# Three element-wise products of an RWKV-7 half on Pool, its bonus weight on ScalarE

## The chip, the cores and the metric

One core of a Trainium2 chip runs the whole program. The metric is the device time in microseconds; the median of several runs of one kernel is compared with that of the other. An engine is named by its usual name or by the profile's: TensorE (PE, with PEld for its weight loads), VectorE (DVE), ScalarE (ACT), Pool (POOL), SyncE (SP).

## What is computed

A two-layer encoder over 256 frames of width 2048: layer 0 mixes tokens with RWKV-7 and Mamba-2 heads side by side, layer 1 with chunked attention, and each ends with a SwiGLU feed-forward. The change touches the RWKV part alone, of which this is the reference, cut:

```python
kk = heads(k * k_k)
kk = kk * lax.rsqrt(jnp.maximum(jnp.sum(kk * kk, axis=-1, keepdims=True), 1e-24))
k = k * (1.0 + (a - 1.0) * k_a)
a_vec = -kk
b_vec = kk * heads(a)
def step(S, inp):
    r_t, w_t, k_t, v_t, a_t, b_t = inp
    sa = jnp.einsum('bhvk,bhk->bhv', S, a_t)
    S = S * w_t[:, :, None, :] + sa[..., None] * b_t[:, :, None, :] + v_t[..., None] * k_t[:, :, None, :]
    return S, jnp.einsum('bhvk,bhk->bhv', S, r_t)
...
bonus = jnp.sum(heads(r) * heads(k) * r_k, axis=-1, keepdims=True) * heads(v)
return (y + bonus.reshape(Bsz, T, RWKV_WIDTH)) * g
```

Here `a` is the in-context rate, `k` the key, `r` the receptance, `r_k` the bonus weight, one number per channel.

## The kernel before

The kernel keeps activations on the chip and streams all weights from HBM in units of 256 x 512 numbers. `stream` (L225 to L243) loads a unit, and for each half of it ScalarE casts a high part `hi` (L240) and VectorE subtracts it to get the low part `lo` (L241). `mm_chunk` (L245) multiplies: for each weight tile and each of two token tiles three matmuls, `hi` by `sh` (L260), `lo` by `sh` (L261), `hi` by `sl` (L262). They are called the streamed matmuls below; `hi_w_in_3_1` is the second half of unit 3 of a chunk. The tiles `hi` and `lo` come from a ring of five, so a cast waits until TensorE has used the tile five places earlier.

The input projection `w_in` has twelve chunks of 512 columns. The RWKV heads are worked in two halves (`rwkv_half`, hf 0 and 1), each with a chunk for key, receptance and value (`which` 0, 1, 2). The chunk's result is evacuated to `tm` by ScalarE, transposed by TensorE to channels by time (`tr`, L424), and mixed with the frame before: ScalarE scales (L429), VectorE adds the shifted part (L430). After the key, ScalarE and VectorE build the rate `a` (128 x 1024), the cumulated decay `c` (its inverse exponential in the end) and the normed key `kk`; L553 to L561 fill the operands `ar` and `bkv`. `bkv` holds per channel and chunk of 64 frames three blocks: the rate-weighted key (L556), the key by rate and decay (L560, L561), the value (L504 to L509). After the receptance, L564 multiplies it into `ar`, L567 forms the bonus product in `r`, and the `aa` matmuls (L576) make the 64 x 64 interactions of four chunks from `bkv` and `ar`; VectorE masks them into `AA` (L580). There are two PSUM banks for `aa`, and each chunk takes both. The triangular inverse follows: VectorE transposes `AA` to `NB` (L591), runs 30 dependent pairs of small instructions (L595, L597), and transposes again to `Sf` and `TG` (L623, L626); then TensorE's `ga` (L634), `gb`, and the recurrence over the chunks (`cx`, `cu`, `ch`, `cy`). The bonus is summed over a head by `bo` (L605). The second half's inverse runs beside the first chunks of the Mamba part (`tr_cv`, L769 convolution steps on VectorE, `xt`, L827 on Pool, `sg`, `yd`).

Each engine runs its instructions in the order in which the framework's scheduler has put them, by priorities (`high_priority`, the stream above the mixer) and its own estimate of durations. An instruction that waits holds all behind it on its engine. Tiles of 128 x 1024 (`r4`) are reused from a pool of nine.

Of the kernel before, what the change touches and what calls it, by code (L numbers as in the profile page):

```python
# [12 lines left out]
AF = mybir.ActivationFunctionType  # L13
ALU = mybir.AluOpType
# [128 lines left out]
def encoder_body(ctx: ExitStack, tc: tile.TileContext, A):  # L143
    nc = tc.nc
    act, dve, pool, pe = nc.scalar, nc.vector, nc.gpsimd, nc.tensor
# [58 lines left out]
    def col(name, i=0, rows=P):  # L204
        return pf[:rows, _PF[name] + i:_PF[name] + i + 1]
# [187 lines left out]
    def mixer0(xt):  # L393
# [5 lines left out]
        with ExitStack() as mx:  # L399
# [76 lines left out]
            def c64(ap):  # L476
                return ap.rearrange("p q (c t) -> p (q c) t", t=64)
# [3 lines left out]
            def rwkv_half(hf):  # L481
                f0 = 4 * hf
# [4 lines left out]
                k = r4(f"k{hf}")  # L487
                r = r4(f"r{hf}")
                bkv = R1.tile([P, 16, 192], F32, tag="bkv", name=f"bkv{hf}")
                for which in range(3):  # L490
                    tm = proj(1 + 3 * hf + which)
                    for q2 in range(2):
                        ps = tr2(tm, [256 * q2, 256 * q2 + 128], P, f"{which}{hf}{q2}")
                        for i in range(2):
                            q = 2 * q2 + i
# [4 lines left out]
                            else:  # L500
# [4 lines left out]
                                               scale=om[:, mi:mi + 1])  # L505
# [4 lines left out]
                                                         op0=ALU.mult, op1=ALU.add)  # L510
                    if which == 0:

                        lw = r4(f"lw{hf}")
                        a = r4(f"a{hf}")
                        for wi, dst in ((0, lw), (1, a)):
                            for q2 in range(2):
                                ps = pra.tile([P, 2, T], F32, tag="ra", name=f"lo{hf}{wi}{q2}")
                                for i in range(2):
                                    q = 2 * q2 + i
                                    pe.matmul(ps[:, i, :], lhsT=w2[:, wi, q * P:(q + 1) * P], rhs=wa[:, wi, :],  # L520
                                              start=True, stop=True)
                                for i in range(2):
                                    q = 2 * q2 + i
                                    b0 = 8 * wi + f0 + q
                                    act.activation(dst[:, q, :], ps[:, i, :], AF.Tanh, scale=0.5,
                                                   bias=hw0[:, b0:b0 + 1])
                        act.activation(lw, lw, AF.Identity, scale=-0.5 * CW, bias=ncw)
                        c = r4(f"c{hf}")
                        for q in range(4):
                            dve.tensor_tensor_scan(c[:, q, :], scan_m, lw[:, q, :], 0.0, op0=ALU.mult, op1=ALU.add)  # L530
                        dve.tensor_tensor(lw, c, lw, op=ALU.subtract)
                        kk = r4(f"kk{hf}")
                        for q in range(4):
                            act.activation(kk[:, q, :], k[:, q, :], AF.Square, scale=col("k_k", f0 + q))
                        for q2 in range(2):
                            ps = pra.tile([P, 2, T], F32, tag="ra", name=f"ss{hf}{q2}")
                            pe.matmul(ps, lhsT=blk, rhs=kk[:, 2 * q2:2 * q2 + 2, :], start=True, stop=True)
                            dve.tensor_scalar(kk[:, 2 * q2:2 * q2 + 2, :], ps, 1e-24, None, op0=ALU.max)
                        act.activation(kk, kk, AF.Ln)
                        act.activation(kk, kk, AF.Exp, scale=-0.5)  # L540
                        for q in range(4):
                            dve.scalar_tensor_tensor(kk[:, q, :], k[:, q, :], col("k_k", f0 + q), kk[:, q, :],
                                                     op0=ALU.mult, op1=ALU.mult)

                        ar = [r4(f"ar{hf}{i}", shape=(P, 8, 128)) for i in range(2)]
                        wt = R2.tile([P, 16], F32, tag="wt", name=f"wt{hf}")
                        act.activation(wt, c64(c)[:, :, 63], AF.Exp)
                        act.activation(lw, lw, AF.Exp)
                        for i in range(2):
                            act.activation(ar[i][:, :, 64:128], c64(c[:, 2 * i:2 * i + 2, :]), AF.Exp)  # L550
                        act.activation(c, c, AF.Exp, scale=-1.0)
                        for i in range(2):
                            dve.scalar_tensor_tensor(ar[i][:, :, 0:64], c64(kk[:, 2 * i:2 * i + 2, :]), -1.0,  # L553
                                                     c64(lw[:, 2 * i:2 * i + 2, :]), op0=ALU.mult, op1=ALU.mult)
                        dve.scalar_tensor_tensor(kk, a, 1.0, kk, op0=ALU.add, op1=ALU.mult)
                        dve.scalar_tensor_tensor(bkv[:, :, 0:64], c64(kk), 0.5, c64(c), op0=ALU.mult, op1=ALU.mult)  # L556
                        for q in range(4):
                            act.activation(a[:, q, :], a[:, q, :], AF.Identity, scale=hka[:, f0 + q:f0 + q + 1],
                                           bias=oka[:, f0 + q:f0 + q + 1])
                        dve.tensor_tensor(a, a, k, op=ALU.mult)  # L560
                        dve.tensor_tensor(bkv[:, :, 64:128], c64(a), c64(c), op=ALU.mult)  # L561
                    elif which == 1:
                        for i in range(2):
                            dve.tensor_tensor(ar[i][:, :, 64:128], c64(r[:, 2 * i:2 * i + 2, :]),  # L564
                                              ar[i][:, :, 64:128], op=ALU.mult)
                        for q in range(4):
                            dve.scalar_tensor_tensor(r[:, q, :], r[:, q, :], col("r_k", f0 + q), a[:, q, :],  # L567
                                                     op0=ALU.mult, op1=ALU.mult)

                        AA = R1.tile([P, 32, 128], F32, tag="AA", name=f"AA{hf}")  # L570
                        for ch in range(4):
                            pss = [pra.tile([P, 4, 128], F32, tag="ra", name=f"aa{hf}{ch}{hp}") for hp in range(2)]
                            for q in range(4):
                                for hp in range(2):
                                    h0 = 64 * hp
                                    pe.matmul(pss[hp][:, q, :], lhsT=bkv[h0:h0 + 64, 4 * q + ch, 0:128],  # L576
                                              rhs=ar[q // 2][h0:h0 + 64, 4 * (q % 2) + ch, :], start=True, stop=True)
                            for hp in range(2):
                                b0 = 8 * ch + 4 * hp
                                dve.tensor_tensor(AA[:, b0:b0 + 4, :], pss[hp],  # L580
                                                  mask_aa[:, None, :].broadcast_to([P, 4, 128]), op=ALU.mult)

                        NBS = r4(f"NB{hf}", shape=(P, 32, 32))
                        NB = NBS[0:64]
                        TG = r4(f"TG{hf}", shape=(64, 32, 32))
                        tmp = R1.tile([64, 256], F32, tag="itmp", name=f"itmp{hf}")

                        for h2 in range(2):
                            b2 = slice(16 * h2, 16 * h2 + 16)
                            act.copy(AA[32:64, b2, 0:32], AA[32:64, b2, 32:64])  # L590
                        dve.transpose(NB, AA[0:64, :, 0:32].rearrange("p b t -> p t b"))  # L591
                        for i in range(1, 31):
                            nt = 31 - i
                            tv = tmp[:, 0:nt * i].rearrange("p (t i) -> p t i", t=nt)
                            inv.tensor_tensor(tv, NB[:, i + 1:32, i:i + 1].broadcast_to([64, nt, i]),  # L595
                                              NB[:, i:i + 1, 0:i].broadcast_to([64, nt, i]), op=ALU.mult)
                            inv.tensor_tensor(NB[:, i + 1:32, 0:i], NB[:, i + 1:32, 0:i], tv, op=ALU.add)  # L597
                        pool.memset(NB.rearrange("p t i -> p (t i)")[:, 0:1024:33], 1.0)
# [4 lines left out]
                for q2 in range(2):  # L603
# [3 lines left out]
                                      op=ALU.mult)  # L607
# [24 lines left out]
                for bb in range(32):  # L632
                    c = bb % 4
# [5 lines left out]
                for bb in range(32):  # L639
                    c = bb % 4  # L640
# [11 lines left out]
                for ch in range(4):  # L652
# [26 lines left out]
                    if ch < 3:  # L679
# [16 lines left out]
                        for hp in range(2):  # L696
                            s = slice(64 * hp, 64 * hp + 64)
                            dve.tensor_tensor(Hn[s, :, s], src[s], wt[s, ch:16:4, None].broadcast_to([64, 4, 64]),
                                              op=ALU.mult)
# [36 lines left out]
                for q2 in range(2):  # L736
# [5 lines left out]
                    for i in range(2):  # L742
                        q = 2 * q2 + i
# [5 lines left out]
                    for i in range(2):  # L749
                        c0 = (2 * q2 + i) * P  # L750
                        for kt in range(2):
# [5 lines left out]
                                      op=ALU.subtract)  # L757
# [239 lines left out]
```

## Time and profile before

| | |
|---|---|
| median of 3 runs | 2372.69 us (2372.19 to 2373.54) |
| the profiled execution | 2376.24 us, its span 2374.5 us |
| mean granted TensorE clock | 0.993 |
| PE busy | 2349.0 us, 99% of the span |
| DVE busy | 1421.5 us, 60% |
| ACT busy | 1273.4 us, 54% |
| POOL busy | 33.0 us, 1% |
| HBM | 180 GB/s over the span |

Busy times are shares of the whole span; the edited lines stand in the first 260 us. Matmuls are pipelined, so a row's duration (some 390 ns for a streamed matmul) is longer than the step from one start to the next. A time such as 88.76 is in microseconds from the span's start. A row of the timeline gives start, duration, engine, line, operation, output and inputs, size, count, and in brackets the idle time before it with what ended it.

### The profile page before, as it was taken

How to read it: one execution, taken by the hardware profiler on the slowest of the kernel's cores; microseconds unless marked ns; L12 is line 12 of the kernel's file. 1: busy time of each engine (PE TensorE's matmuls, PEld its weight loads, DVE VectorE, ACT ScalarE, POOL GpSimd, SP SyncE). 2: the span in 40 equal slices, each digit the busy share in tenths (PEclk: the TensorE clock that was granted, in tenths of full speed). 3: DMA queues.
4: the chain of work that ended last, by engine and by line, in shares of the span. 5: the costliest groups of instructions: out<-in, count | busy, mean ns of one | idle time of the engine just before them, and what ended most of it. 6: DMA issues, size and time to landing. Idle time of an engine off the chain costs nothing.

```text
span 2374.5 us, 31651 instructions
## 1 busy us (share of the span) xinstructions
PE 2349.0 (99%) x11426; PEld 1921.0 (81%) x11426; DVE 1421.5 (60%) x2376; ACT 1273.4 (54%) x2260; POOL 33.0 (1%) x61
## 2 busy tenths in 40 slices
PE   9999999999999999999999999999999999999998
PEld 7777777878888888888878888887888888888887
DVE  6867968675555555555556555557555555555554
ACT  7647546665554454454446555556545445445443
POOL 0000000000000000000000000000000000000000
PEclk9999989999999999999999999999999999999999
DMA  7434424666666666666666655566666666666664
GB/s 243 148 110 137 140 87 157 207 180 193 186 191 191 187 192 189 188 197 200 196 196 187 191 174 167 171 193 181 193 186 191 190 187 192 189 187 197 201 194 148
DMA packets 119357, 429.17 MB, mean 181 GB/s; under 512 B 13408, under 2 KB 13664, under 8 KB 119200
## 3 DMA queue, kind: packets, MB, share of 16 engines
q1 hardware_dynamic: 115280, 415.35, 57.8%
q0 software_dynamic: 2400, 9.18, 1.5%
q10 hardware_dynamic: 1520, 2.63, 0.3%
q8 instruction: 89, 1.46, 0.3%
q14 instruction: 68, 0.56, 0.1%
HBM read 425.01 MB, written 2.10 MB: 180 GB/s over the span
## 4 chain that ended last, share of the span: by engine, by line
PE 93%; DVE 4%; ACT 1%; issue 1%; DMA 1%; POOL 0%; DVEq 0%; SPq 0%; ACTq 0%; POOLq 0%
PE mm_w_gu L260 13%; PE mm_w_gu L261 13%; PE mm_w_gu L262 13%; PE mm_w_dn L260 7%; PE mm_w_dn L262 7%; PE mm_w_dn L261 7%; PE mm_w_qkv L260 4%; PE mm_w_qkv L261 4%; PE mm_w_qkv L262 4%; PE mm_w_in L262 3%; PE mm_w_in L260 2%; PE mm_w_in L261 2%; DVE lo_w_in L241 1%; PE mm_w_oc L261 1%; PE mm_w_oc L260 1%; PE mm_w_oc L262 1%
## 5 line engine op out<-in xcount | busy, mean ns | idle before, releaser
L241 DVE TENSOR_TENSOR lo_w_gu<-raw_w_gu,hi_w_gu 128x512 fp32r<-128x512 f32 x704 | 485.8, 691 | 417.4 <-ACT hi_w_gu L240 414.9
L240 ACT CAST hi_w_gu<-raw_w_gu 128x512 fp32r<-128x512 f32 x704 | 438.5, 624 | 452.7 <-DVE lo_w_gu L241 404.9
L261 PE MATMUL mm_w_gu<-lo_w_gu,sh_f 128*128 128x512 f32 x1408 | 550.0, 391 | 0.0
L260 PE MATMUL mm_w_gu<-hi_w_gu,sh_f 128*128 128x512 f32 x1408 | 549.3, 390 | 0.7 <-ACT sh_f L299 0.5
L262 PE MATMUL mm_w_gu<-hi_w_gu,sl_f 128*128 128x512 f32 x1408 | 548.5, 390 | 0.0
L241 DVE TENSOR_TENSOR lo_w_dn<-raw_w_dn,hi_w_dn 128x512 fp32r<-128x512 f32 x352 | 242.8, 691 | 221.6 <-ACT hi_w_dn L240 221.2
L240 ACT CAST hi_w_dn<-raw_w_dn 128x512 fp32r<-128x512 f32 x352 | 219.0, 624 | 248.3 <-DVE lo_w_dn L241 237.7
L260 PEld LDWEIGHTS mm_w_gu<-hi_w_gu,sh_f 128*128 128x128 f32 x1408 | 264.3, 188 | 58.1 <-ACT sh_f L299 3.4
L262 PEld LDWEIGHTS mm_w_gu<-hi_w_gu,sl_f 128*128 128x128 f32 x1408 | 264.4, 188 | 55.4 <-DVE sl_f L300 1.2
L261 PEld LDWEIGHTS mm_w_gu<-lo_w_gu,sh_f 128*128 128x128 f32 x1408 | 264.4, 188 | 54.0 <-DVE lo_w_gu L241 0.3
L261 PE MATMUL mm_w_dn<-lo_w_dn,hh 128*128 128x512 f32 x704 | 274.0, 389 | 0.0
L262 PE MATMUL mm_w_dn<-hi_w_dn,hl 128*128 128x512 f32 x704 | 274.0, 389 | 0.0
L260 PE MATMUL mm_w_dn<-hi_w_dn,hh 128*128 128x512 f32 x704 | 273.9, 389 | 0.0
L241 DVE TENSOR_TENSOR lo_w_qkv<-raw_w_qkv,hi_w_qkv 128x512 fp32r<-128x512 f32 x192 | 132.3, 691 | 104.6 <-ACT hi_w_qkv L240 104.1
L240 ACT CAST hi_w_qkv<-raw_w_qkv 128x512 fp32r<-128x512 f32 x192 | 119.0, 621 | 110.3 <-DVE lo_w_qkv L241 64.8
L260 PE MATMUL mm_w_in<-hi_w_in,sh_in 128*128 128x512 f32 (+1 forms) x384 | 155.7, 406 | 1.7 <-ACT hi_w_in L240 1.7
L261 PE MATMUL mm_w_in<-lo_w_in,sh_in 128*128 128x512 f32 (+1 forms) x384 | 156.5, 408 | 0.0
L262 PE MATMUL mm_w_in<-hi_w_in,sl_in 128*128 128x512 f32 (+1 forms) x384 | 156.1, 406 | 0.0
L262 PEld LDWEIGHTS mm_w_dn<-hi_w_dn,hl 128*128 128x128 f32 x704 | 132.2, 188 | 27.4
L260 PEld LDWEIGHTS mm_w_dn<-hi_w_dn,hh 128*128 128x128 f32 x704 | 132.2, 188 | 27.3
L261 PEld LDWEIGHTS mm_w_dn<-lo_w_dn,hh 128*128 128x128 f32 x704 | 132.2, 188 | 27.3
L262 PE MATMUL mm_w_qkv<-hi_w_qkv,sl_qkv 128*128 128x512 f32 x384 | 151.5, 394 | 0.0
(351 smaller groups left out, 2778.8 us busy)
## 6 DMA issues: line engine op xcount, KB each, us to landing
raw_w_gu<-in_w_gu SPq DMA_DIRECT2D x352, 512.0 KB, 3.6
raw_w_dn<-in_w_dn SPq DMA_DIRECT2D x176, 512.0 KB, 4.2
raw_w_qkv<-in_w_qkv SPq DMA_DIRECT2D x96, 512.0 KB, 3.6
raw_w_in<-in_w_in SPq DMA_DIRECT2D x92, 512.0 KB, 3.6
raw_w_oab<-in_w_oab SPq DMA_DIRECT2D x32, 512.0 KB, 4.2
raw_w_oc<-in_w_oc SPq DMA_DIRECT2D x32, 512.0 KB, 4.2
bias<-in_bias POOLq DMA_DIRECT2D x4, 768.0 KB, 6.9
x_in<-in_x SPq DMA_DIRECT2D x4, 512.0 KB, 8.9
```

Source lines behind the costliest of these rows:

```text
L240: act.copy(hi, raw[:, h, :])
L241: dve.tensor_tensor(lo, raw[:, h, :], hi.bitcast(F32), op=ALU.subtract)
L260: pe.matmul(o, lhsT=xh, rhs=h_[:, :width], start=k_ == 0, stop=False)
L261: pe.matmul(o, lhsT=xh, rhs=l_[:, :width], start=False, stop=False)
L262: pe.matmul(o, lhsT=xl, rhs=h_[:, :width], start=False, stop=k_ == nk - 1)
```

## The change

In each of the two halves the product of rate and key, the product of that with the inverse decay, and the product of receptance and rate key go from VectorE to Pool. The factor `r_k`, before a column factor of the receptance product on VectorE, is now multiplied into `a` in place by four ScalarE instructions ahead of it. What is computed stays the same.

```diff
-                        dve.tensor_tensor(a, a, k, op=ALU.mult)
-                        dve.tensor_tensor(bkv[:, :, 64:128], c64(a), c64(c), op=ALU.mult)
+                        pool.tensor_tensor(a, a, k, op=ALU.mult)
+                        pool.tensor_tensor(bkv[:, :, 64:128], c64(a), c64(c), op=ALU.mult)
+                        for q in range(4):
+                            act.activation(a[:, q, :], a[:, q, :], AF.Copy, scale=col("r_k", f0 + q))
                     elif which == 1:
                         for i in range(2):
                             dve.tensor_tensor(ar[i][:, :, 64:128], c64(r[:, 2 * i:2 * i + 2, :]),
                                               ar[i][:, :, 64:128], op=ALU.mult)
-                        for q in range(4):
-                            dve.scalar_tensor_tensor(r[:, q, :], r[:, q, :], col("r_k", f0 + q), a[:, q, :],
-                                                     op0=ALU.mult, op1=ALU.mult)
+                        pool.tensor_tensor(r, r, a, op=ALU.mult)
```

In the changed kernel the scalings are L563, the products of receptance and decay L566 (L564 before), the bonus product L568. The scheduler moves other instructions along. Three places follow; numbers at the end of a name tell buffers apart.

ScalarE in the first half, from the last cast of unit 2 of the value chunk on, before:

```order
L240 CAST hi_w_in_2_1_1105<-raw_w_in_2_1099 128x512
L429 ACTIVATE r_467<-tr_913,om 128x256
L429 ACTIVATE r_467<-tr_922,om 128x256
L240 CAST hi_w_in_3_0_1123<-raw_w_in_3_1121 128x512
L240 CAST hi_w_in_3_1_1127<-raw_w_in_3_1121 128x512
```

and now:

```order
L240 CAST hi_w_in_2_1_1106<-raw_w_in_2_1100 128x512
L563 ACTIVATE a_669<-a_669,pf 128x256 x4
L240 CAST hi_w_in_3_0_1124<-raw_w_in_3_1122 128x512
L429 ACTIVATE r_467<-tr_917,om 128x256
L429 ACTIVATE r_467<-tr_926,om 128x256
L240 CAST hi_w_in_3_1_1128<-raw_w_in_3_1122 128x512
```

The four scalings of `a` and a cast now stand ahead of the evacuations of the receptance.

VectorE in the second half, from the last receptance mix to the first masks of `aa`, before:

```order
L430 SCALAR_TENSOR_TENSOR r_1661<-tr_2116,pf,r_1661 128x255
L567 SCALAR_TENSOR_TENSOR r_1661<-r_1661,pf,a_1863 128x256
L241 TENSOR_TENSOR lo_w_in_6_0_2989<-raw_w_in_6_2986,hi_w_in_6_0_2988 128x512
L564 TENSOR_TENSOR ar_1909<-r_1661,ar_1909 128x8x64
L567 SCALAR_TENSOR_TENSOR r_1661<-r_1661,pf,a_1863 128x256 x3
L580 TENSOR_TENSOR AA_2131<-aa_2132,cc 128x512
L580 TENSOR_TENSOR AA_2131<-aa_2133,cc 128x512
```

and now:

```order
L430 SCALAR_TENSOR_TENSOR r_1662<-tr_2121,pf,r_1662 128x255
L241 TENSOR_TENSOR lo_w_in_4_0_2947<-raw_w_in_4_2944,hi_w_in_4_0_2946 128x512
L566 TENSOR_TENSOR ar_1909<-r_1662,ar_1909 128x8x64
L566 TENSOR_TENSOR ar_1910<-r_1662,ar_1910 128x8x64
L241 TENSOR_TENSOR lo_w_in_4_1_2951<-raw_w_in_4_2944,hi_w_in_4_1_2950 128x512
L506 SCALAR_TENSOR_TENSOR bkv_1663<-tr_2430,pf,bkv_1663 128x3x64
L509 SCALAR_TENSOR_TENSOR bkv_1663<-tr_2430,pf,bkv_1663 128x63
L580 TENSOR_TENSOR AA_2133<-aa_2134,cc 128x512
L580 TENSOR_TENSOR AA_2133<-aa_2135,cc 128x512
```

The masks come two units of the weight stream earlier, and a `lo` and two mixes of the value now stand directly ahead of them. On ScalarE the cast `hi_w_in_4_1`, which that `lo` needs, stands behind the four scalings. On TensorE the transposes of the value stand 13 streamed matmuls earlier than before, behind five of the six of `hi_w_in_2_0`.

TensorE at `ga` of the second half, in the first Mamba value chunk, before:

```order
L262 MATMUL mm_w_in_1_3369<-hi_w_in_6_1_3508,sl_in_129 128x512
L634 MATMUL ga_2520<-TG_2181,AA_2131 32x32 x32
L260 MATMUL mm_w_in_0_3368<-hi_w_in_7_0_3526,sh_in_128 128x512
L261 MATMUL mm_w_in_0_3368<-lo_w_in_7_0_3527,sh_in_128 128x512
L262 MATMUL mm_w_in_0_3368<-hi_w_in_7_0_3526,sl_in_129 128x512
L818 MATMUL xt_3289<-cc,xf_3078 128x128 x4
```

and now:

```order
L262 MATMUL mm_w_in_0_3370<-hi_w_in_3_0_3440,sl_in_125 128x512
L634 MATMUL ga_2522<-TG_2183,AA_2133 32x32 x32
L260 MATMUL mm_w_in_1_3371<-hi_w_in_3_0_3440,sh_in_124 128x512
L261 MATMUL mm_w_in_1_3371<-lo_w_in_3_0_3441,sh_in_124 128x512
L262 MATMUL mm_w_in_1_3371<-hi_w_in_3_0_3440,sl_in_125 128x512
```

`ga` stands 45 streamed matmuls earlier, and `xt` follows it 30 streamed matmuls later instead of 3. On VectorE 112 instructions instead of 124 run from the transpose into `NB` to the one into `TG`: 5 `lo` and 7 convolution steps (L769) fewer.

## Rows read from the trace of the kernel before

**Rows 1.** The page, part 1: busy time, share of the span, instructions.

```profile
PE 2349.0 (99%) x11426; PEld 1921.0 (81%) x11426; DVE 1421.5 (60%) x2376; ACT 1273.4 (54%) x2260; POOL 33.0 (1%) x61
```

**Rows 2.** TensorE's waits, 80 to 320 us: total, times, longest.

```profile
PE ga L634 <- DVE TG L626: 3.2, 2, 1.8
PE tr L424 <- DVE r L430: 2.2, 1, 2.2
PE tr L424 <- ACT tm L416: 1.5, 1, 1.5
PE xt L818 <- DVE xf L780: 1.2, 1, 1.2
```

**Rows 3.** Windows: stretch, then busy time (instructions) of each engine, clock, DMA.

```profile
core 0: us, PE busy (x) PEld busy (x) DVE busy (x) ACT busy (x) POOL busy (x), PEclk, DMA share, GB/s
...
234.00:246.00 12.00, 9.80 (x57) 7.43 (x56) 12.00 (x22) 6.53 (x13) 0.98 (x2) 1.00 0.64 196
145.00:165.00 20.00, 18.15 (x207) 12.51 (x205) 9.88 (x14) 9.47 (x17) 0.94 (x1) 0.74 0.31 85
310.00:335.00 25.00, 22.42 (x220) 16.19 (x219) 16.52 (x21) 11.23 (x20) 5.14 (x3) 0.66 0.30 85
```

**Rows 4.** Timeline of the first half, 82 to 116 us, all engines.

```profile
88.02 0.60 ACT L558 ACTIVATE a<-a,oka,hka 128x256 f32<-128x256 f32 x1
...
88.76 1.22 DVE L560 TENSOR_TENSOR a<-a,k 128x1024 f32<-128x1024 f32 x1
...
90.92 0.84 ACT L429 ACTIVATE r<-tr,om 128x256 f32<-128x256 f32 x2
...
95.15 0.69 DVE L564 TENSOR_TENSOR ar<-r,ar 128x512 f32<-128x512 f32 x1
...
96.17 0.71 PE L576 MATMUL aa<-ar,bkv 64*128 64x128 f32 x8
...
97.59 1.67 DVE L567 SCALAR_TENSOR_TENSOR r<-r,pf,a 128x256 f32<-128x256 f32 x4
...
100.16 1.50 PE L576 MATMUL aa<-ar,bkv 64*128 64x128 f32 x16
```

**Rows 5.** Timeline of Pool.

```profile
311.53 0.94 POOL L625 MEMSET Sf<- 32x1024 f32 x1 [6.56 <-ACT Sf L624]
312.57 2.03 POOL L827 TENSOR_TENSOR L<-cc,adt 128x1024 f32<-128x1024 f32 x1
...
384.53 2.28 POOL L827 TENSOR_TENSOR L<-cc,adt 128x1024 f32<-128x1024 f32 x1 [39.18 <-DVE lo_w_in L241]
394.23 1.90 POOL L827 TENSOR_TENSOR L<-cc,adt 128x1024 f32<-128x1024 f32 x1 [7.43 <-PE yd L839]
```

**Rows 6.** Groups of ScalarE, 60 to 110 us: busy us, mean ns, idle before.

```profile
L534 ACT ACTIVATE kk<-k,pf 128x256 f32<-128x256 f32 x4 | 2.0, 516 | 0.0
```

**Rows 7.** Timeline of VectorE beside two products of Pool.

```profile
313.39 1.75 DVE L241 TENSOR_TENSOR lo_w_in<-raw_w_in,hi_w_in 128x512 fp32r<-128x512 f32 x1
...
394.19 0.69 DVE L841 TENSOR_TENSOR xs<-xs,yd 128x512 f32<-128x512 f32 x1 [0.89 <-PE yd L839]
```

**Rows 8.** Timeline of the second half, ScalarE, TensorE and VectorE.

```profile
234.35 1.09 ACT L558 ACTIVATE a<-a,oka,hka 128x256 f32<-128x256 f32 x2
...
240.75 0.63 PE L424 MATMUL tr<-cc,tm 128*128 128x128 f32 x4 [2.20 <-DVE r L430]
...
253.83 1.27 DVE L580 TENSOR_TENSOR AA<-aa,cc 128x512 f32<-128x512 f32 x2
...
256.74 0.39 PE L262 MATMUL mm_w_in<-hi_w_in,sl_in 128*128 128x512 f32 x1
```

**Rows 9.** Timeline of TensorE around the second `ga`; a group of VectorE, 255.7 to 313 us.

```profile
310.63 0.39 PE L260 MATMUL mm_w_in<-hi_w_in,sh_in 128*128 128x512 f32 x1
...
311.77 0.39 PE L262 MATMUL mm_w_in<-hi_w_in,sl_in 128*128 128x512 f32 x1
313.55 0.75 PE L634 MATMUL ga<-TG,AA 32*32 32x32 f32 x64 [1.40 <-DVE TG L626]
...
L769 DVE SCALAR_TENSOR_TENSOR xf<-tr_cv,hcv,xf 128x255 f32<-128x255 f32 (+2 forms) x12 | 5.6, 470 | 0.0
```

## The prediction

> **What bounds the kernel now.** The page comes first: TensorE is busy for 2349.0 of 2374.5 us [rows 1]. The reader is to see that a microsecond saved on VectorE is worth something only where TensorE waits for it. So I read next TensorE's waits over the stretch of the two RWKV halves [rows 2]. Four kinds matter: `ga` behind VectorE's transpose `TG` (3.2 us in two waits), `tr` behind VectorE's `r` (2.2), `tr` behind ScalarE's `tm` (1.5), `xt` behind `xf` (1.2). That is 8.1 us, nearly all that a relieved VectorE could give back directly. [...]
>
> **What the change adds and removes.** Per half VectorE loses 1.22 + 1.22 us (two key products of one size) and 1.67 us (four receptance products) [rows 4], 4.1 us, 8.2 in all. Pool gains three 128x1024 products. The nearest Pool row is L827, a product of the same size: 1.90 to 2.28 us [rows 5]; its operands are broadcast, where the new ones are full tiles and one is written with a stride. I bound them by 1.2 (the same product on VectorE) and 2.4 (twice that), and take 2.1, the middle of the nearest rows. ScalarE gains four 128x256 scalings per half; four of that shape with a column scale took 2.0 us [rows 6].
>
> **VectorE's relief is mostly taken back.** During L827 the trace shows what a VectorE product does beside Pool [rows 5, 7]. The `lo` subtraction at 313.39 reads two SBUF tiles. It took 1.75 us and ended at 315.14, 0.54 us after Pool's product (312.57 + 2.03 = 314.60). L841, of the same size, reads PSUM and one SBUF tile, and took 0.69 us beside Pool's product of 394.23. So I take it that a two-tile VectorE instruction that meets a Pool product stands until Pool is done; and that Pool waits for one in progress, which may be why L827 spreads from 1.90 to 2.28. Three Pool products per half can hold up to 6.3 us of VectorE for the 4.1 us freed.
>
> **First half: a new wait on ScalarE.** The bonus weight scales `a` in place, so it must wait until Pool's second product has read `a`; in the new order it stands ahead of the next weight cast and of all four `r` evacuations. `a` is complete at 88.02 + 0.60 = 88.62 [rows 4]. Pool's two products and 0.3 us for VectorE subtractions in progress bring 93.1; the four scalings 95.2; the cast 95.8. The first `r` evacuation, at 90.92 before, starts 4.9 us later. From it to the end of the first L564 took 4.9 us before, with a key product in between; by the new order (evacuations, two casts, L430, three `lo`) I count 3.9, so it ends at 99.7 instead of 95.84. The `aa` matmuls followed 0.33 us behind (96.17), so now 100.0. The new order gives TensorE only six streamed matmuls more ahead of them (6 x 0.228; from 310.63 to 311.77 are five such steps [rows 9]), which end at 97.4: a gap of 2.6 us. The second chunk of `aa` then starts at 103.0 instead of 100.16, since VectorE no longer has the 1.67 us in between. TensorE and the inverse chain both lose **2.8 us**.
>
> **Second half.** `a` is complete at 234.35 + 1.09 = 235.44 [rows 8]. Pool's first product runs 235.6 to 237.5 and holds `lo_w_in_3_1`, so the third `r` mix ends at 238.5, where before it released TensorE at 240.75. But the transposes of `v`, which wait for it, now stand 13 streamed matmuls earlier: TensorE reaches them at 235.4 and waits 3.2 us (2.20 before [rows 8]). Pool's second product ends at 239.9 and holds `lo_w_in_4_0`; the first L566 follows, done at 241.05, and `aa` starts at 241.35, another 1.1 us. ScalarE is blocked by the scalings until 242.0, the cast `hi_w_in_4_1` comes at 242.6, its `lo` meets Pool's third product (242.1 to 244.0) and ends at 244.55, and only behind it and two `v` mixes does VectorE empty the first `aa` banks, at 245.7. The second `aa` chunk starts at 246.0; TensorE was ready at 243.3, so 2.7 us more. Carried on at the old pace, the last mask product ends at 253.9 (253.83 + 1.27 = 255.10 before), and TensorE, with `bo` done and the same streamed work behind it, stands at 259.6 instead of 256.7. **Plus 3.0 us** for TensorE; the inverse chain starts 1.2 us earlier.
>
> **The end of that chain.** In the new order 5 `lo` and 7 convolution steps fewer lie between the transposes `NB` and `TG` (0.69, as L564 of that size, and 0.47 us each, and some 0.08 less where they overlap [rows 4, 9]): 5.8 us. `TG`, which let `ga` start at 313.55, is then done at 313.5 - 1.2 - 5.8 = 306.5. But `ga` also stands 45 streamed matmuls earlier: TensorE is there at 312.0 - 10.2 + 3.0 = 304.8 and waits 1.7 us, 1.4 before [rows 9]. **Plus 0.3.** `xt` now has 30 streamed matmuls behind `ga` instead of 3, so its wait goes: **minus 1.2**. Sum of the waits: 2.8 + 3.0 + 0.3 - 1.2 = **4.9 us**.
>
> **The clock.** The first wait for `TG` (1.8 us) and the second with that for `xf` behind it (1.40 and 1.2) came just before the two low stretches; the gap of 2.20 at 240.7 brought none (1.00 in its window [rows 3]). The change adds gaps of 2.6, 3.2, 1.1 and 2.7. One new fall is what I expect. Ten microseconds at half rate cost 5 if TensorE has work all the time and nothing if it waits anyway; the `aa` phase is half waits, so 2.5 us, bounds 0 and 5 each.
>
> **Pool's start.** [...] Before, L827 began 0.1 us behind the memset ahead of it (311.53 + 0.94 to 312.57 [rows 5]), so I add nothing.
> [...]
>
> **Forecast: 4.9 + 2.5 = 7.4 us slower.** The profiled execution took 2376.24 us (span 2374.5), 3.55 over the median of 2372.69; taken against the median this gives **2380 us**. A measurement here can tell 0.2%, 4.7 us, from no change.
>
> **Rivals.**
> - *The blocks cost less.* Pool at 1.9 us, no new fall, and the gap of the second half absorbed by an earlier chain: 2.4 + 1.5 - 1.2, about 2.5 us, 2375. For it: 2.20 us of gap at 240.7 left the clock up. Against it: the blocked scalings stand ahead of casts and evacuations in both halves, so two gaps at least must shrink at once. Chance 0.26.
> - *Faster: VectorE's relief decides.* If Pool finds room between VectorE's instructions and the second inverse chain ends 7 us earlier or more, `ga` no longer waits (-1.4), `xt` neither (-1.2), and the fall of 17 us behind them stays out (up to -8.5); against the 2.8 + 3.0 that leaves -5.3, 2367.4. It decides from the point where `TG` is done before TensorE reaches `ga`, which is 1.7 us away by my count. Chance 0.09.
> - *Much slower.* Pool needs 2.4 us or more on full tiles, and the clock falls in both halves by the full price: 4.9 + 2 x 0.6 + 2 x 5 = 16 us, 2389; with half the price of the falls 11 us, 2384. Chance 0.13.
> [...]
> - That the change doesn't do what it says is out: the order shows the three products on Pool in both halves.
>
> **How the numbers follow.** The forecast has 0.50. Slower by over 0.2% are the forecast, the third rival and the fourth, 0.65; within 0.2% the first, 0.26; faster the second, 0.09. The range leaves out the faster case and the upper part of the much slower one: 2373 to 2387. The forecast's own range, with a fall at 0 to 5 us, is 2377.5 to 2383.
>
> **What would show it.** Right: a ScalarE wait of 2 us or more for Pool ahead of L563 in both halves, `aa` in the first half 3 to 4 us later and behind a TensorE gap over 2 us, `lo` rows of 1.5 to 2.5 us beside L560, L561 and L568, a new low stretch of the clock near 100 or 240 us, and times equal from some 400 us on but for the shift. Wrong: Pool rows near 1.2 us, `r` evacuations that don't move, or a `ga` in the second half without a wait.

## The result and the profile after

| | before | after |
|---|---|---|
| median (6 runs each) | 2373.14 us (2372.19 to 2375.99) | 2390.00 us (2386.05 to 2394.01) |
| ratio | | 1.0066, 95% interval 1.0053 to 1.0079 |
| profiled execution | 2376.24 us, span 2374.5 | 2394.00 us, span 2392.2 |

The change makes the kernel 17 us slower, more than twice the 7.4 us forecast and above the range. The page of the changed kernel, part 1, answers to [rows 1]:

```profile
PE 2356.7 (99%) x11426; PEld 1926.0 (81%) x11426; DVE 1425.3 (60%) x2364; ACT 1275.4 (53%) x2268; POOL 48.2 (2%) x67
```

VectorE has twelve instructions fewer and is busy 3.8 us longer. The timeline of Pool shows most of the reason (L560 and L561 are the key products, L568 the bonus product). VectorE's rows beside these products follow in a second table:

```profile
88.44 2.36 POOL L560 TENSOR_TENSOR a<-a,k 128x1024 f32<-128x1024 f32 x1 [22.79 <-ACT a L558]
90.88 2.73 POOL L561 TENSOR_TENSOR bkv<-a,c 128x1024 f32<-128x1024 f32 x1
101.30 2.69 POOL L568 TENSOR_TENSOR r<-r,a 128x1024 f32<-128x1024 f32 x1 [7.69 <-DVE ar L566]
...
242.81 2.38 POOL L560 TENSOR_TENSOR a<-a,k 128x1024 f32<-128x1024 f32 x1 [22.90 <-ACT a L558]
245.27 2.70 POOL L561 TENSOR_TENSOR bkv<-a,c 128x1024 f32<-128x1024 f32 x1
249.87 2.37 POOL L568 TENSOR_TENSOR r<-r,a 128x1024 f32<-128x1024 f32 x1 [1.89 <-DVE ar L566]
```

```profile
88.89 5.26 DVE L241 TENSOR_TENSOR lo_w_in<-raw_w_in,hi_w_in 128x512 fp32r<-128x512 f32 x2 [0.32 <-ACT hi_w_in L240]
...
243.68 2.05 DVE L241 TENSOR_TENSOR lo_w_in<-raw_w_in,hi_w_in 128x512 fp32r<-128x512 f32 x1
245.66 0.86 DVE L430 SCALAR_TENSOR_TENSOR r<-tr,pf,r 128x255 f32<-128x255 f32 x2
246.45 2.08 DVE L241 TENSOR_TENSOR lo_w_in<-raw_w_in,hi_w_in 128x512 fp32r<-128x512 f32 x1
...
250.25 2.53 DVE L241 TENSOR_TENSOR lo_w_in<-raw_w_in,hi_w_in 128x512 fp32r<-128x512 f32 x1 [0.53 <-ACT hi_w_in L240]
```

Each of the five subtractions that meet a Pool product ends 0.54 to 0.56 us behind it (243.68 + 2.05 = 245.73 against 242.81 + 2.38 = 245.19; the row at 88.89 holds two of them, of 2.45 and 2.89 us). Such a wait of a VectorE instruction for a Pool product is called a hold below. Without a Pool product such a row takes 0.68 (86.85, 97.29), so the holds cost 3.9 us in the first half and 4.6 in the second, 8.5 in all, for the 8.2 that VectorE was to be relieved of. The two L430, which read PSUM and one SBUF tile, ran beside L561 at 0.43 each. The waits of TensorE from 80 to 330 us (the list of [rows 2], without one of 0.4 us for a DMA):

```profile
PE aa L576 <- DVE ar L566: 4.0, 2, 2.8
PE tr L424 <- DVE r L430: 3.3, 1, 3.3
PE ga L634 <- DVE TG L626: 3.2, 2, 1.8
PE aa L576 <- DVE AA L580: 2.3, 1, 2.3
PE gb L641 <- DVE TG L637: 1.6, 1, 1.6
PE tr L424 <- ACT tm L416: 1.5, 1, 1.5
PE bt L614 <- DVE bv L606: 1.3, 2, 0.6
```

They make 17.2 us. The kernel before had the 8.1 of [rows 2] and one more, which that list leaves out:

```profile
PE bt L614 <- DVE bv L606: 1.0, 2, 0.6
```

So there were 9.1 us before, and 8.1 are new. And the clock (windows, columns as in [rows 3]: the granted clock stands behind POOL's busy time), before:

```profile
95.00:115.00 20.00, 20.00 (x124) 15.68 (x123) 17.69 (x35) 7.41 (x12) 0.99 (x2) 1.00 0.39 116
145.00:170.00 25.00, 23.15 (x276) 16.19 (x275) 11.98 (x18) 10.63 (x20) 0.94 (x1) 0.80 0.29 86
240.00:270.00 30.00, 28.88 (x178) 21.56 (x179) 28.29 (x66) 15.59 (x28) 0.98 (x2) 1.00 0.37 111
310.00:340.00 30.00, 27.42 (x286) 20.63 (x285) 18.12 (x24) 12.22 (x22) 5.14 (x3) 0.72 0.26 72
```

and after:

```profile
95.00:115.00 20.00, 17.24 (x99) 13.02 (x98) 13.40 (x22) 7.52 (x15) 4.55 (x5) 0.83 0.35 106
145.00:170.00 25.00, 23.18 (x212) 16.92 (x212) 14.33 (x29) 11.19 (x19) 1.09 (x2) 0.73 0.36 106
240.00:270.00 30.00, 22.89 (x115) 16.81 (x113) 23.51 (x35) 11.62 (x24) 9.31 (x7) 0.83 0.29 87
310.00:340.00 30.00, 26.98 (x245) 19.71 (x243) 22.70 (x40) 14.81 (x25) 3.14 (x3) 0.77 0.37 109
```

The lower of the two levels is half of full speed in these traces: before was granted 0.50 in each microsecond from 152 to 161 and from 316 to 332, after from 255 to 265. Streamed matmuls start there every 0.43 us (257.40, 257.82, 258.25 of after) instead of every 0.23 (242.00, 242.23, 242.45). So twice one less the clock, times the stretch, is the time at that level: 0 to 6.8 us, 10.0 to 13.5, 0 to 10.2, 16.8 to 13.8. That is 17.5 us more in these four stretches, worth up to half of it, 8.7. The page divides the 17.7 us between the two spans otherwise: TensorE is busy 7.7 us longer for the same 11426 matmuls, and so idle 10.0 us longer. The 8.1 us of new waits are most of the second part; a lower clock fits the size of the first.

The runs say the same without a trace, since each has its mean granted clock. Before took 2379.4 us at 0.991, 2376.4 at 0.993 and 2372.9 at 0.995 (1, 7 and 6 of the 27 runs of one comparison). The six runs of after took 2394.0 at 0.988, 2391.4 at 0.989, 2394.0 at 0.990 (the profiled one), 2388.6 at 0.991 and twice 2386.1 at 0.993. So 0.001 of clock is some 1.6 us in either kernel, with runs up to 3 us off that line. At the same clock the change costs 9.2 us (0.991, one run each) or 9.7 (0.993): about what the new waits come to. The other 7 us go with a lower clock.

### The profile page after: what moved, and what is told of

It is laid out like the page before. It is cut to its first block, busy times and chain, and to the rows that moved or that the text cites. A ratio compares the mean times of both kernels' runs of the same rounds, so it can differ in the third digit from the quotient of the medians.

```text
span 2392.2 us, 31669 instructions
## 1 busy us (share of the span) xinstructions
PE 2356.7 (99%) x11426; PEld 1926.0 (81%) x11426; DVE 1425.3 (60%) x2364; ACT 1275.4 (53%) x2268; POOL 48.2 (2%) x67
## 4 chain that ended last, share of the span: by engine, by line
PE 94%; DVE 3%; ACT 1%; issue 1%; DMA 1%; POOL 1%; SPq 0%; DVEq 0%; POOLq 0%; ACTq 0%
PE mm_w_gu L260 13%; PE mm_w_gu L262 13%; PE mm_w_gu L261 13%; PE mm_w_dn L262 7%; PE mm_w_dn L261 7%; PE mm_w_dn L260 7%; PE mm_w_qkv L260 4%; PE mm_w_qkv L261 4%; PE mm_w_qkv L262 4%; PE mm_w_in L262 3%; PE mm_w_in L260 3%; PE mm_w_in L261 3%; PE mm_w_oc L261 1%; PE mm_w_oab L262 1%; PE mm_w_oab L261 1%; PE mm_w_oc L260 1%
## 5 line engine op out<-in xcount | busy, mean ns | idle before, releaser
L241 DVE TENSOR_TENSOR lo_w_gu<-raw_w_gu,hi_w_gu 128x512 fp32r<-128x512 f32 x704 | 486.1, 691 | 417.1 <-ACT hi_w_gu L240 414.6
L241 DVE TENSOR_TENSOR lo_w_dn<-raw_w_dn,hi_w_dn 128x512 fp32r<-128x512 f32 x352 | 243.0, 692 | 221.4 <-ACT hi_w_dn L240 221.0
L241 DVE TENSOR_TENSOR lo_w_qkv<-raw_w_qkv,hi_w_qkv 128x512 fp32r<-128x512 f32 x192 | 132.3, 691 | 104.5 <-ACT hi_w_qkv L240 104.1
L241 DVE TENSOR_TENSOR lo_w_in<-raw_w_in,hi_w_in 128x512 fp32r<-128x512 f32 x184 | 135.4, 744 | 47.2 <-ACT hi_w_in L240 46.3
L240 ACT CAST hi_w_in<-raw_w_in 128x512 fp32r<-128x512 f32 x184 | 112.5, 618 | 88.7 <-PE mm_w_in L262 76.8
```

The costliest lines, as they stand in the source:

```text
L240: act.copy(hi, raw[:, h, :])
L241: dve.tensor_tensor(lo, raw[:, h, :], hi.bitcast(F32), op=ALU.subtract)
```

## The experiments

The medians below stand against runs of the kernel before on the same chip (2374.1 to 2376.3 us). Not all experiments ran on one chip, so one is best compared with another by the ratios.

**Which part of the change.** Four kernels keep parts of it; the edits stand against the change. The third leaves the factor `r_k` out of the bonus.

```diff
@@ e1_key_only @@
-for q in range(4):
-    act.activation(a[:, q, :], a[:, q, :], AF.Copy, scale=col("r_k", f0 + q))
...
-pool.tensor_tensor(r, r, a, op=ALU.mult)
+for q in range(4):
+    dve.scalar_tensor_tensor(r[:, q, :], r[:, q, :], col("r_k", f0 + q), a[:, q, :],
+                             op0=ALU.mult, op1=ALU.mult)
@@ e2_bonus_only @@
-pool.tensor_tensor(a, a, k, op=ALU.mult)
-pool.tensor_tensor(bkv[:, :, 64:128], c64(a), c64(c), op=ALU.mult)
+dve.tensor_tensor(a, a, k, op=ALU.mult)
+dve.tensor_tensor(bkv[:, :, 64:128], c64(a), c64(c), op=ALU.mult)
@@ e3_no_scale @@
-for q in range(4):
-    act.activation(a[:, q, :], a[:, q, :], AF.Copy, scale=col("r_k", f0 + q))
@@ e4_scale_r @@
-for q in range(4):
-    act.activation(a[:, q, :], a[:, q, :], AF.Copy, scale=col("r_k", f0 + q))
...
+for q in range(4):
+    act.activation(r[:, q, :], r[:, q, :], AF.Copy, scale=col("r_k", f0 + q))
 pool.tensor_tensor(r, r, a, op=ALU.mult)
```

> The key products stay on Pool, the bonus product goes back to VectorE as it was, and the four scalings on ScalarE go with it. Theory 1 (ScalarE's block: the scalings wait for Pool's second product and hold the receptance evacuations and casts behind them, and the gaps which that opens lower the clock): nothing on ScalarE waits for Pool, the evacuations of r start near 90.9 us as before, no gap over 2 us before aa in the first half, no clock fall near 100 us, 2373 to 2378 us. Theory 2 (Pool's products hold VectorE, in an order that reckons with a free VectorE): the subtractions beside L560 and L561 still take 2 to 3 us, gaps of 2 us or more stay in the second half and most of the cost stays, 2380 to 2388 us.

> The key products stay on VectorE; only the scalings on ScalarE and the bonus product on Pool are kept. Theory 1: the scalings wait for VectorE's second key product, done near 91.3 us in place of 93.6, so the block is some 2 us shorter; a gap under 1 us before aa, 2374 to 2379 us. Theory 2: one Pool product in a half holds VectorE instead of three, a third of the 17 us, 2376 to 2381 us. This kernel tells the two apart only together with the first: theory 1 wants this one slower than the first, theory 2 faster.

> The change with the four scalings left out, so that the bonus lacks the factor r_k; all three products stay on Pool. Theory 1: as the kernel with the key products alone, 2373 to 2379 us, and the first half's aa at 95 to 97 us. Theory 2: the three holds of 2.4 to 2.9 us per half stay, TensorE waits 2 us or more in the second half before the transposes of the value, the clock falls there, 2382 to 2390 us.

> The change with r_k multiplied into r in place, after the products of receptance and decay, instead of into a after the key products: the same work on each engine, but ScalarE waits for VectorE's L566 instead of for Pool's L561. Theory 1: the evacuations of r come first again, so the gap before aa in the first half goes; a shorter wait for L566 holds one or two casts, 2374 to 2380 us. Theory 2: as with the scalings left out, 2382 to 2390 us.

| | median us | ratio to before |
|---|---|---|
| e1_key_only | 2388.90 | 1.0063 (1.0050 to 1.0075) |
| e2_bonus_only | 2378.64 | 1.0016 (1.0007 to 1.0025) |
| e3_no_scale | 2383.91 | 1.0037 (1.0025 to 1.0050) |
| e4_scale_r | 2386.54 | 1.0050 (1.0037 to 1.0063) |

Theory 1, that ScalarE's block is the cause, falls with the first kernel: no scaling is left and nearly all of the cost is. Its two largest waits of TensorE are those of the change:

```profile
PE aa L576 <- DVE ar L564: 3.6, 2, 2.6
PE tr L424 <- DVE r L430: 3.3, 1, 3.3
```

The gap before `aa` needs no scalings: with Pool's key products alone the scheduler puts the first `aa` five streamed matmuls earlier than before, and VectorE, held by L560 and L561 (again 5.26 us for two subtractions), comes later. Theory 2 had the other three right, and the first 1 us too low. The second alone lies in the range of either theory, but it is faster than the first, which theory 2 asked for and theory 1 did not. The change without its scalings (the third) is about 6 us faster than the change. That is not shown to be the price of ScalarE's block: the first kernel has no scalings either, and is 5 us slower than the third.

**The hold.** The first kernel again (the edits stand against it), with Pool's products once in quarters and once all but left out: in the second, 60 of every 64 frames of that part of the key operand stay zero.

```diff
@@ e5_split @@
-pool.tensor_tensor(a, a, k, op=ALU.mult)
-pool.tensor_tensor(bkv[:, :, 64:128], c64(a), c64(c), op=ALU.mult)
+for q in range(4):
+    pool.tensor_tensor(a[:, q, :], a[:, q, :], k[:, q, :], op=ALU.mult)
+    pool.tensor_tensor(bkv[:, 4 * q:4 * q + 4, 64:128], ...)
@@ e6_relief @@
+pool.memset(bkv[:, :, 64:128], 0.0)
...
-pool.tensor_tensor(a, a, k, op=ALU.mult)
-pool.tensor_tensor(bkv[:, :, 64:128], c64(a), c64(c), op=ALU.mult)
+pool.tensor_tensor(c64(a)[:, :, 0:4], c64(a)[:, :, 0:4], c64(k)[:, :, 0:4], op=ALU.mult)
+pool.tensor_tensor(bkv[:, :, 64:68], c64(a)[:, :, 0:4], c64(c)[:, :, 0:4], op=ALU.mult)
```

> The kernel with the key products alone on Pool, each cut into four products of 128x256. Theory 2 as it now stands: a VectorE subtraction stands until the Pool product that it meets is done, so with pieces of some 0.6 to 0.7 us it is let in after at most 0.7; its rows fall from 2.0 to 2.9 us to 1.4 or less, and the two chains, Pool's and VectorE's, now share what one of them waited for: the gap before aa in the first half shrinks from 2.7 to 1 us or less, 2379 to 2385 us. If the hold lasts as long as Pool has any product in its queue, or if the moved order alone makes the gaps, nothing changes: 2386 to 2391 us.

> The kernel with the key products alone on Pool, with each product done for four frames of 64 only, and the rest of the key operand set to zero before the key is there: the key by rate and decay is left out for the other frames. VectorE keeps the relief of 2.4 us per half, and Pool holds it for some 0.2 us in place of 5. If the hold is the cause, the subtractions take 0.7 us again, the gaps of 2.7 and 3.5 us shrink to 1 or less and the time is at most the one before, 2366 to 2374 us. If the moved order is the cause whatever Pool takes, it stays at 2383 us or more. If VectorE's relief is worth nothing, 2372 to 2375.

Quarters took 2386.26 us (1.0049, 1.0035 to 1.0063), the relief 2377.73 (1.0013, 1.0004 to 1.0022). The timeline of the second, Pool and then VectorE:

```profile
88.52 0.31 POOL L561 TENSOR_TENSOR a<-a,k 128x64 f32<-128x64 f32 x1 [22.79 <-ACT a L559]
88.91 0.32 POOL L562 TENSOR_TENSOR bkv<-a,c 128x64 f32<-128x64 f32 x1
```

```profile
88.98 0.80 DVE L241 TENSOR_TENSOR lo_w_in<-raw_w_in,hi_w_in 128x512 fp32r<-128x512 f32 x1 [0.32 <-ACT hi_w_in L240]
```

Without the long products the gap before the first `aa` is gone, at the same place in TensorE's order, and 12 of the 15 us go with it. That prices the hold, with the gap and the fall behind it. What is left shows that VectorE's relief bought nothing here: 2.4 us less work per half, and still 2 to 3 us slower than before. With quarters a subtraction takes 1.21 us at most and the gap before `aa` in the first half shrinks from 2.6 to 0.9 us, as expected, but now Pool's pieces are slow beside VectorE's work:

```profile
86.91 2.21 POOL L561 TENSOR_TENSOR a<-a,k 128x256 f32<-128x256 f32 x1 [20.28 <-ACT a L558]
...
93.42 0.74 POOL L562 TENSOR_TENSOR bkv<-a,c 128x256 f32<-128x256 f32 x1
94.13 0.73 POOL L561 TENSOR_TENSOR a<-a,k 128x256 f32<-128x256 f32 x1
94.94 1.06 POOL L562 TENSOR_TENSOR bkv<-a,c 128x256 f32<-128x256 f32 x1
```

The eight pieces last from 86.91 to 96.00, 9.1 us where the two products took 5.2, and in the second half `aa` waits 0.9 us for Pool itself. The time came down by less than 3 us. It missed the range expected by one and lies in that of the other line (2386 to 2391), though the rows rule out the first reason given there: the hold did get shorter.

**The order.** `behind(x, (matrix, chunk, weight tile, token tile))` adds an edge of issue order only: x stands on TensorE behind the first matmul on that tile. All else of the change stays, and the scheduler arranges the rest around it.

```diff
@@ e7_order @@
+behind(aa_of(0), ("w_in", 3, 7, 1))
+behind(tr_of("210") + tr_of("211"), ("w_in", 7, 6, 1))
+behind(aa_of(1), ("w_in", 7, 8, 1))
@@ e10_order2 @@
+behind(aa_of(0), ("w_in", 3, 7, 1))
+behind(tr_of("210"), ("w_in", 7, 7, 0))
+behind(tr_of("211"), ("w_in", 7, 11, 1))
+behind(aa_of(1), ("w_in", 7, 10, 1))
+behind(ga_of(0), ("w_in", 5, 2, 1))
+behind(ga_of(1), ("w_in", 9, 14, 1))
```

These edits too stand against the change. Of e7_order's three lines e11_order_first has the first alone, e12_order_second the other two.

> The change, with TensorE's order alone moved back by hand: the first aa of the first half stands 9 streamed matmuls later, the transposes of the value in the second half 9 and more, the first aa of the second half 17 and more; the scheduler moves ga along. All Pool and ScalarE work stays. If TensorE only meets these steps too early while streamed work is at hand, the gaps of 2.9, 3.5, 1.4 and 2.5 us go, the clock stays up behind them and the time falls by 8 us or more, to 2374 to 2382. If VectorE is too late as a whole (the held subtractions delay the streamed matmuls and the chain to TG as well), the gaps come back as waits for lo or later at ga, 2384 to 2392 us.

> The change with TensorE's order moved back in the first half only (first aa 10 streamed matmuls later). The kernel with both halves moved back is 13 us faster than the change. If each gap costs its own length and its fall of the clock, this one gains the 2.9 us gap and the fall at 101 us, some 5 to 7 us: 2383 to 2386 us, the remaining gaps of the second half as in the change (3.5, 1.4, 2.5). If one half alone carries the cost, it is 2376 to 2380 or still 2389 to 2392.

> The change with TensorE's order moved back in the second half only (transposes of the value 13 and more streamed matmuls later, the first aa 22). By the same reckoning the gaps of 3.5, 1.4 and 2.5 us shrink to one of some 4 us, and of the two falls behind them one stays: 2382 to 2386 us, and the gap of 2.9 us with its fall at 101 us remains. If the parts don't add up, the sum of the gains of the two is well over or under 13 us.

> The change, with TensorE's order moved back by hand further: the second transposes of the value stand behind the tile where VectorE's held receptance mix was ready, aa of the second half behind the fifth unit, and ga of both halves later. All Pool and ScalarE work stays. If the cost of the change is only that TensorE meets these steps before the held VectorE has them, the waits of 4.3 us (transposes) and 1.9 and 1.5 us (ga) go: 2366 to 2372 us, the time of the kernel before with ga later. If the held VectorE costs by itself, 2373 to 2379 us, and the waits stand at other places.

| | median us | ratio to before |
|---|---|---|
| e7_order | 2376.82 | 1.0012 (1.0003 to 1.0020) |
| e11_order_first | 2378.48 | 1.0016 (1.0007 to 1.0025) |
| e12_order_second | 2388.29 | 1.0051 (1.0039 to 1.0064) |
| e10_order2 | 2382.82 | 1.0028 (1.0018 to 1.0039) |

With TensorE's steps moved later, 13 of the 17 us go, though every Pool product is still there and VectorE is still held for 8.7 us in e7_order's profile. Two of its rows (L243 and L570 there are L241 and L566 of the change):

```profile
89.30 5.26 DVE L243 TENSOR_TENSOR lo_w_in<-raw_w_in,hi_w_in 128x512 fp32r<-128x512 f32 x2 [0.32 <-ACT hi_w_in L242]
...
245.58 2.82 DVE L570 TENSOR_TENSOR ar<-r,ar 128x512 f32<-128x512 f32 x1
```

So the cost takes both: a VectorE that is held, and an order in which TensorE comes to its results too early. Take either away and most of it goes. Too early doesn't always mean earlier than in the kernel before. With the key products alone `aa` of the first half stands five streamed matmuls earlier; in the change it stands six later, but VectorE's results come later still. Ten more in e7_order and e11_order_first left a wait of 0.5 us.

Most of the gain comes with the line for the first half (11.5 us by the medians, 11.9 by the ratios) and little with the other two (1.7 and 3.6). The 5 to 7 us and 4 to 8 first expected missed on both sides; the other line of e11_order_first's expectation, one half that carries the cost, had 2376 to 2380. Not all of the 11.5 lies at 97 us, though: the scheduler moved the second half's steps along, and in the profile the clock over 145 to 170 us is 0.93 instead of 0.73, over 310 to 340 us 0.89 instead of 0.77. So this run doesn't price the gap at 97 us by itself.

In the second half e7_order did not do what was expected: TensorE waits 4.2 us for the second transposes of the value. There later isn't better, and e10_order2, which went furthest, missed both its ranges. Behind VectorE's held steps the gap only moves, to the second chunk of `aa`, which waits for the masks; e12_order_second and e10_order2 in turn:

```profile
PE aa L580 <- DVE AA L584: 5.3, 1, 5.3
```

```profile
PE aa L580 <- DVE AA L584: 3.7, 2, 3.5
```

**The kernel before, with its own gaps moved.**

```diff
@@ e8_ga_later @@
+behind(ga_of(0), ("w_in", 5, 1, 1))
+behind(ga_of(1), ("w_in", 9, 15, 1))
@@ e9_ga_xt_later @@
+behind(ga_of(0), ("w_in", 5, 1, 1))
+behind(ga_of(1), ("w_in", 9, 15, 1))
+behind([("xt", 0, t, q) for t in range(2) for q in range(4)], ("w_in", 10, 2, 1))
```

> The kernel before, with its two waits for TG taken away by order: ga of the first half stands behind the second weight tile of its chunk (7 streamed matmuls later), ga of the second half behind the last tile but one half (10 later), and xt behind it. Nothing else is edited. The gaps of 2.0, 1.6 and 1.4 us go, 5 us. If the falls of the clock at 151 and 315 us come from these gaps, they stay out and give another 3 to 8 us: 2360 to 2367 us and a mean granted clock of 0.997 or more. If the clock falls for another reason, 2367 to 2371 us with the same falls.

> The kernel before with ga of both halves later, and with the transposes xt of the first Mamba value chunk moved too, by 18 or more streamed matmuls, so that the wait for xf of 3.2 us, which the last of these kernels had put in place of the one for TG, goes as well. If gaps there lower the clock, the fall at 317 us stays out: 2365 to 2370 us, clock 0.997. If that fall comes without a gap, 2369 to 2372.

They took 2372.16 us (0.9988, 0.9979 to 0.9997) and 2372.78 (0.9987, 0.9978 to 0.9996): both beat the kernel before by some 3 us, which is less than hoped and under 0.2%. The fall of the clock at 151 us stays out; in the second half the wait went from `TG` to `xf` (3.2 us), then to `gb` (3.3), and the fall stayed, if shorter (0.83, then 0.89, instead of 0.72). Windows of e8_ga_later:

```profile
145.00:170.00 25.00, 24.19 (x298) 16.83 (x296) 14.98 (x25) 12.32 (x23) 0.94 (x2) 1.00 0.37 122
310.00:340.00 30.00, 26.79 (x309) 19.62 (x307) 19.38 (x25) 12.26 (x22) 4.87 (x3) 0.83 0.27 82
```

**The clock by itself.** Useless matmuls fill the gaps and leave the waits as they are. The line, written out, is that of the first `aa`; the others are alike, on a free bank where the awaited one is not free.

```diff
@@ e13_fill_after @@
+for j in range(12):
+    pe.matmul(pss[0], lhsT=st[0][0][:, 0, 0:P], rhs=st[0][0][:, 0:2, :], start=True, stop=True)
```

> The change, with useless matmuls of 128x512 placed on TensorE where it waits: 12 ahead of the first aa of the first half, 13 ahead of the transposes of the value and 5 ahead of the first aa in the second half; their results are overwritten or not read. The waits behind them stay as long as they were, so they take no time from TensorE that it has. If the falls at 101 and 255 us come from these gaps, they stay out or get shorter and the change is 4 to 8 us faster, 2382 to 2386. If the falls come from elsewhere (the aa phase itself, or chance), 2388 to 2392, or more where the filling overruns the wait.

> The kernel before, filled in the same way: 14 useless matmuls of 128x256 ahead of ga of the first half, 11 ahead of ga of the second, 9 of 128x512 ahead of the transposes of the value in the second half; the wait for xf isn't filled. If the gaps cause the falls, the one at 151 us stays out, that at 315 us stays out or is shorter: 2368 to 2373 us at a clock of 0.996 or more. If not, 2373 to 2377 with the falls as before.

Neither median moved: 2389.96 us (1.0063, 1.0048 to 1.0078) and 2375.34 (0.9998, 0.9990 to 1.0007). The profile of the first:

```profile
98.19 2.88 PE L491 MATMUL aa<-sh_in 128*128 128x512 f32 x12
101.12 0.71 PE L593 MATMUL aa<-ar,bkv 64*128 64x128 f32 x8
```

```profile
95.00:115.00 20.00, 19.56 (x121) 15.48 (x120) 14.95 (x24) 9.16 (x19) 4.54 (x5) 1.00 0.37 106
240.00:270.00 30.00, 26.61 (x132) 19.71 (x130) 21.74 (x41) 10.36 (x22) 9.36 (x7) 0.77 0.19 60
```

In the first half the filling ends where `aa` can start, and the clock stays at 1.00. From the first chunk of `aa` to the fourth it is 7.5 us there (101.12 to 108.63) and 10.3 in the change (100.10 to 110.41), which has one streamed matmul more in between: that fall is worth some 2.5 us. In the second half the wait of 1.6 us for the masks wasn't filled, and behind it the clock fell for longer than in the change (0.77, where the change has 0.83).

The profiled execution took 2387.9 us, 6 less than that of the change. But the six runs average a clock of 0.992, with 0.991 in the change, which by the price above is some 2 us, and the medians are the same. Why they don't show the first half's gain isn't settled.

In the second kernel's profile the fall at 151 us stays out (1.00 over 145 to 170 us). The one at 315 us stays (0.77 over 310 to 340 us), where the wait for `xf`, 1.3 us, wasn't filled; and a short one has come near 240 us behind 1.3 us for `r`.

Over the sixteen profiles gap and fall go together in the first half. With a gap of 2.6 to 2.8 us before the first `aa`, the clock over 95 to 115 us was under 1.00 in four of five (0.74 to 0.91; e3_no_scale kept 1.00); without one of that size it was 1.00 in all eleven. With a gap of 1.6 to 1.9 us before the first half's `ga` it was under 1.00 over 145 to 170 us in eleven of twelve, without it in none of four. A gap doesn't lower the clock each time, but without one it didn't fall there at all. In the second half the tie is looser: 2.2 us at 240.7 in the kernel before brought no fall, and the 1.3 us just named did.

## Why the prediction was wrong

- **What bounds the kernel, and the hold:** right. TensorE bounds the kernel (busy for 2356.7 of 2392.2 us), two-tile subtractions stood beside Pool (2.05 to 2.89 us, 0.68 without it), the two L430, which read PSUM, didn't (0.43), and the relief was taken back whole (8.5 us of holds for 8.2).
- **The Pool product at 2.1 us:** mis-sized. It took 2.36 to 2.38 for L560, 2.70 to 2.73 for L561 with its strided output, 2.37 and 2.69 for L568; three of the six are over the upper bound of 2.4, the others just under it. In the second half the working itself took less than the 2.1 that it names, 1.9 for the first product and the third (235.6 to 237.5, 242.1 to 244.0).
- **The first half's wait:** right, as ScalarE's row and TensorE's show:

```profile
93.64 1.71 ACT L563 ACTIVATE a<-a,pf 128x256 f32<-128x256 f32 x4 [3.12 <-POOL bkv L561]
```

```profile
100.10 0.72 PE L576 MATMUL aa<-ar,bkv 64*128 64x128 f32 x8 [2.76 <-DVE ar L566]
```

  ScalarE's scalings waited 3.1 us and started at 93.64 (forecast 93.1), TensorE reached `aa` at 97.3 and started it at 100.10 behind a gap of 2.76 (97.4, 100.0 and 2.6). That the scalings were the reason was only part of it: without them, `aa` stands earlier and the gap is 2.6.
- **The second half's waits:** right one by one, wrong in sum. The rows of TensorE:

```profile
246.19 1.09 PE L424 MATMUL tr<-cc,tm 128*128 128x128 f32 x8 [3.35 <-DVE r L430]
249.27 1.23 PE L576 MATMUL aa<-ar,bkv 64*128 64x128 f32 x16 [1.28 <-DVE ar L566]
253.95 2.50 PE L576 MATMUL aa<-ar,bkv 64*128 64x128 f32 x16 [2.35 <-DVE AA L580]
258.81 2.67 PE L576 MATMUL aa<-ar,bkv 64*128 64x128 f32 x16
263.41 2.22 PE L576 MATMUL aa<-ar,bkv 64*128 64x128 f32 x16
```

  Forecast were 3.2, 1.1 and 2.7, which is 4.8 more than before; the step "carried on at the old pace" turned that into 3.0. There was no old pace: the last two rows take 2.67 and 2.22 us where such a chunk took 1.50 [rows 4], at a granted clock of 0.50 up to 265 us. The credit of 1.2 for `xt` came true, but `gb` waits 1.6 in its stead. So 8.1 us of new waits, not 4.9.
- **"One new fall is what I expect", 2.5 us:** this step failed most. Two new falls came, behind the gaps of both halves, the one near 155 us got longer, and in the runs the clock is worth some 7 us. The price that I put on a fall was right (some 2.5 measured, in the first half); the number was not. I let one row (2.20 us of gap at 240.7, clock up) weigh as much as the two waits for `TG`, shorter than that, each of which had a fall behind it, and so took one fall for four gaps. The ten microseconds at half rate are what the first low stretch of [rows 3] comes to (2 x 0.26 x 20), and the fall of 17 us the second (2 x 0.34 x 25); the trace grants 0.50 in both, from 152 to 161 and from 316 to 332 us.
- **The rivals:** "much slower", with Pool at 2.4 us or more and the clock down in both halves, is nearest to what happened, and at 0.13 it was held too cheap. That its 16 us nearly met the 17 measured is in part luck: it put 6.1 on the waits and the products and 10 on the clock, where 8 to 10 and 7 to 9 were found, and three of the six products stayed under 2.4. The faster one needed `TG` early: `ga` of the second half still waits 1.4 us. The fourth, a late first product on Pool at 0.02, didn't come: `a` was complete at 88.35 (87.75 + 0.60) and Pool began at 88.44, 0.1 us later.

## What to carry to other kernels

Moving a two-tile product from a busy VectorE to Pool relieved nobody here (8.5 us of holds for 8.2 us of work), since VectorE had two-tile work of its own beside it: count the hold, which is what is left of the Pool product, against the time saved. A scheduler that takes the relief as given also puts the consumers earlier, or not late enough, and that turns a hold into idle time of the engine that bounds the kernel. And where that engine is TensorE, price each new gap twice: its length, and a likely fall of the clock behind it, as with the gaps of 1.6 to 2.8 us in the first half here, behind 15 of 17 of which the granted clock fell (0.73 to 0.93 in the windows).

## What was not expected of the hardware

A Pool product cut in four (e5_split) got slower, not only finer: pieces of 0.73 us took up to 1.30 beside VectorE, and the first of each half 2.21 and 2.74. The same Pool product with the same shapes took 2.37 and 2.69 us in different places. And six runs of one kernel spread over 8 us (2386 to 2394), mostly in step with the mean granted clock (0.993 to 0.988), so that a single time of such a kernel says little about a change of 0.2%.
